# One norm of a hybrid backbone: squares summed two and two, and the latent stream's last residual put ahead of the context stream's last operand blocks

## The chip, the cores and the metric

The kernel runs on one core of a Trainium2 chip, in one launch. The metric is the device time of that launch in microseconds (us). PE is TensorE (matmul), DVE is VectorE (elementwise work and reductions), ACT is ScalarE (activations and copies), POOL is GpSimd, SP is SyncE; the last two mainly issue DMAs here. Each engine works through its own instructions in the order in which they stand, and waits on the others by semaphores.

## The reference

The network has four layers. Each holds a token mixer (layers 0 and 3 a gated DeltaNet, layer 1 differential attention, layer 2 an mLSTM) and a squared-ReLU MLP, and runs over two streams of 256 tokens with 1024 channels: the context and the latent tokens. After each of the two, a stream is updated and normalised:

```
xl = layer_norm(ALPHA * xl + m_lat[2] * yl, ln_g[i, 0], ln_b[i, 0])
xl = layer_norm(ALPHA * xl + m_lat[5] * sq_relu_mlp(modulate(xl, m_lat[3], m_lat[4]), w1[i], w2[i]),
                ln_g[i, 1], ln_b[i, 1])
if need_ctx:
    xc = layer_norm(ALPHA * xc + m_ctx[2] * yc, ln_g[i, 0], ln_b[i, 0])
    xc = layer_norm(ALPHA * xc + m_ctx[5] * sq_relu_mlp(...), ln_g[i, 1], ln_b[i, 1])

def layer_norm(x, g, b):
    mu = mean(x, -1);  var = mean(square(x - mu), -1)
    return (x - mu) * rsqrt(var + LN_EPS) * g + b
```

In layer 3 the context stream is no longer needed (`need_ctx` is false). So six places normalise both streams (two in each of the layers 0, 1 and 2), and two places in layer 3 normalise the latent stream alone.

## The kernel before

Activations lie transposed: 128 channels on the partitions, tokens along the free dimension, so a stream is 8 blocks of 128 x 256, and both streams side by side are 512 columns. All weights are split into a high and a low part, and so are the operands; a product is three passes of the PE (high x high, high x low, low x high; L201 to L203 for both streams together, L251 for one stream of 256 columns).

An output projection with its norm is `out_norm` (L706). Its first four output blocks run over both streams at once. The last four (`KEEP`) keep their weights and run once for the context half and then once for the latent half: `half(0)` and `half(1)`, 4 blocks x 8 input blocks x 3 passes = 96 passes each (L251). Each finished block is added to the residual `xa` (`residual`, L607), and summed into `acc` for the mean.

The norm is a generator, `layer_norm` (L615). It yields numbers, and `beside` (L699) puts that many passes of a fill between its steps. While the context norm is written, the fill is `half(1)`, the latent half of the same projection. While the latent norm is written, the fill is the context half of the next projection's first four blocks (`proj_first`, L221), again 96 passes. After that the latent half of those blocks follows. So the PE's order is fixed by hand in this region (`manual_schedule`), and what the norm needs from DVE and ACT must be ready when the PE comes to it.

The steps of one norm are: the mean, two matmuls against a matrix of 1/1024, one with `acc` (L620) and one with the last block of `xa` (L622); four subtractions of the mean, each over two blocks (128 x 512); four squares on ACT (L645); a sum of the squares on DVE; the variance, matmuls of the summed squares against the same matrix (L652); rsqrt by ACT and DVE; and then `emit_h` (L558), which makes the next projection's operands in four pairs of blocks p = 0 to 3: multiply by r (`xa<-xa,rs`), scale and shift (`hh`, `hf` on ACT and DVE), and the low part (`hl<-hf,hh`). The low part of pair p is written after the multiply and the scale of pair p + 1.

These DVE instructions all go through `dve` (L691), which chains each behind the one before, in the order in which the Python code issues them. They all stand at line L694 in the profile, so tile names tell them apart. The generator `norm(1, first)` gets the rest of the context norm as `other`: what the context norm had not issued when the fill ran out is issued inside the latent norm, after its four subtractions.

`NORM` holds the numbers that are yielded: `NORM[2]` = 12 passes between the mean and the subtractions, `NORM[6]` = 18 before the variance, `NORM[5]` = 20 before the operands, `NORM[4]` = 12 after each pair of operands. `VADD` says which of the four squares take in the one before: with 1, 2 and 3 all four end in one sum. Outside such regions a scheduler with a timeline of its own orders the instructions.

Of the kernel before, what the change touches and what calls it, by code (L numbers as in the profile page):

```python
# [62 lines left out]
APRI = 200  # L63
STAGS = "sds"
RPRI = 100
NORM = 0, 1, 12, 0, 12, 20, 18
VADD = 1, 2, 3
HACT = 1,
RACT = 1,
TAGS = "dddo"  # L70
# [50 lines left out]
class Net:  # L121
# [436 lines left out]
    def emit_h(self, xs, p0, s, aff, act, r=None, step=2):  # L558
# [3 lines left out]
        def low(t, hi, lo):  # L562
            for i in range(0, 2, step):
                e = slice(i, i + step)
                self.behind[1:] = [self.dve("tensor_tensor", out=lo[:, e], in0=t[:, e], in1=hi[:, e].bitcast(F32), op=ALU.subtract)]

        todo = None
        for p, x in enumerate(xs, p0):
# [16 lines left out]
            todo = t, hi, lo  # L585
            yield NORM[4]
        low(*todo)
# [27 lines left out]
    def layer_norm(self, li, lnk, s, acc, aff, act, spill=None, other=(), alone=False):  # L615

        nc = self.nc
        mu = self.ps("mu", "s")[:, CTX]
        yield NORM[0]
        nc.tensor.matmul(mu, self.onesd, acc, start=True, stop=False)  # L620
        yield NORM[1]
        nc.tensor.matmul(mu, self.onesd, self.xs(s, 7), start=False, stop=True)  # L622
        var = self.ps("var", "s")[:, CTX]
        blocks = lambda t, n: t.rearrange("p (b t) -> p b t", b=n)
        over = lambda t, n: t.unsqueeze(1).to_broadcast([P, n, NS])
        yield NORM[2]
        step = 1 if alone else 2
        for b in range(0, 8, step):
            x = blocks(self.xs(s, b, step), step)
            self.dve("tensor_tensor", out=x, in0=x, in1=over(mu, step), op=ALU.subtract)  # L630
        for _ in other:
            pass
        if alone:
            for b in range(8):
                if b % 4 == 0:
                    sqs = self.u("sq")
                sq = sqs[:, NS * (b % 4):NS * (b % 4 + 1)]
                nc.scalar.activation(sq, self.xs(s, b), AF.Square)
                nc.tensor.matmul(var, self.onesd, sq, start=b == 0, stop=b == 7)  # L639
                yield 1  # L640
        else:
            sq = [self.u("sq") for _ in range(2)]
            sq = [t[:, c] for t in sq for c in (LO, HI)]
            for p in range(4):
                nc.scalar.activation(sq[p], self.xs(s, 2 * p, 2), AF.Square)  # L645
                if p in VADD:
                    self.dve("tensor_tensor", out=sq[p], in0=sq[p - 1], in1=sq[p], op=ALU.add)
            ps = [p for p in range(4) if p + 1 not in VADD]
            for n, p in enumerate(ps):
                yield NORM[3] if n < len(ps) - 1 else NORM[6]  # L650
                for i in range(2):
                    nc.tensor.matmul(var, self.onesd, sq[p][:, STREAM[i]], start=p == ps[0] and i == 0, stop=p == 3 and i == 1)  # L652

        rt = self.u("rs", NT)
        r, t = rt[:, CTX], rt[:, LAT]
        nc.scalar.activation(r, var, AF.Ln, bias=self.bias[LN_EPS])
        nc.scalar.activation(r, r, AF.Exp, scale=-0.5)
        nc.scalar.activation(t, r, AF.Square)
        self.dve("scalar_tensor_tensor", out=t, in0=var, scalar=LN_EPS, in1=t, op0=ALU.add, op1=ALU.mult)
        self.dve("scalar_tensor_tensor", out=r, in0=t, scalar=-3.0, in1=r, op0=ALU.add, op1=ALU.mult)  # L660
        yield NORM[5]
        base = (li * 2 + lnk) * 8
        if act is None:
            for b in range(8):
                x = self.xs(s, b)
                nc.vector.scalar_tensor_tensor(out=x, in0=x, scalar=self.lng[:, base + b:base + b + 1], in1=r, op0=ALU.mult, op1=ALU.mult)
                nc.scalar.activation(x, x, AF.Identity, bias=self.par("ln_b", base + b))
                nc.sync.dma_start(out=self.out[:, b], in_=x)
        else:
            yield from self.emit_h([self.xs(s, b, 2) for b in range(0, 8, 2)], 0, s, aff, act, r, step)  # L670

        def rest(i):

            with ExitStack() as q:
                for e in self.behind:
                    q.enter_context(self.tc.issue_after(e))
                for b in range(4 * i, 4 * i + 4):
                    x = self.xs(s, b)
                    g, c = (a[:, base + b:base + b + 1] for a in (self.lnag, self.lnab))
                    if b % 2 in RACT:  # L680
                        nc.scalar.activation(x, x, AF.Identity, bias=c, scale=g)
                    else:
                        nc.vector.tensor_scalar(out=x, in0=x, scalar1=g, scalar2=c, op0=ALU.mult, op1=ALU.add)
                if spill is not None:
                    nc.gpsimd.dma_start(out=spill[:, 4 * i:4 * i + 4, STREAM[s]], in_=blocks(self.xs(s, 4 * i, 4), 4))

        if act is not None:
            for i in range(2):
                self.later(1 + i, rest, i)
# [1227 lines left out]
```

## Time and profile before

| | |
|---|---|
| time, three runs | 2708.55, 2710.31, 2710.56 us; median 2710.31 |
| the profiled execution | 2708.96 us, of which its span is 2707.1 |
| PE busy | 2529.4 us (93% of the span) |
| DVE busy | 1756.8 us (65%) |
| ACT busy | 1302.3 us (48%) |
| PE waits for `mu` on DVE (`xa`) | 16.7 us in six waits |
| PE waits for `var` on DVE (`sq`) | 11.2 us in ten waits |
| mean granted PE clock | 0.97 of full speed |

Matmuls are pipelined, so a row's duration is longer than the step to the next row: 128 x 256 passes last 0.28 us and start every 0.12 us. What counts on the PE is the time from one start to the next. A wait is the idle time of an engine in front of an instruction, put down to what ended last before it. The granted clock is 1.00 at 2.4 GHz and 0.50 at 1.2 GHz.

### The profile page before, as it was taken

Reading aid. Unit: us, or ns where it says so; the run is one execution under the profiler, and the core shown is the slowest. Engines: PE = TensorE matmul, PEld = TensorE weight load, DVE = VectorE, ACT = ScalarE, POOL = GpSimd, SP = SyncE. Lnnn points to the kernel's source line nnn. Section 1 sums busy time; section 2 is a strip of 40 time slices with the busy share of each in tenths; the row PEclk is TensorE's granted clock in tenths of the full one; section 3 lists DMA queues with packets and bytes.
Section 4 is the critical chain, followed back from the end, with each engine's and each line's share of the span. In section 5 each row is a group of like instructions: output and inputs, shape, how many; then the busy total and the mean of one; then the engine's idle time right before and its main releaser. Section 6 shows DMA issues by size and latency. Waiting matters only on the chain. (4 is left out here: it accounts for less than half of the span.)

```text
span 2707.1 us, 40474 instructions
## 1 busy us (share of the span) xinstructions
PE 2529.4 (93%) x15596; PEld 2101.9 (78%) x15596; DVE 1756.8 (65%) x3697; ACT 1302.3 (48%) x2521; POOL 180.5 (7%) x319
## 2 busy tenths in 40 slices
PE   8998798999999997999999999899999998878998
PEld 4776697887788765888778877788888876677997
DVE  4798867656646556775664546575554778866555
ACT  4545485533245345543324534362254554546654
POOL 0110020000000000000000000000021011001000
PEclk9998899999999998999999999999999998999999
DMA  7576342354541321244544134324498277533454
GB/s 275 186 266 208 113 149 94 125 163 156 162 145 65 133 102 63 94 128 160 159 160 140 63 135 155 116 80 150 143 344 318 79 248 285 216 131 125 130 185 131
DMA packets 118418, 424.86 MB, mean 157 GB/s; under 512 B 13512, under 2 KB 15560, under 8 KB 118224
## 3 DMA queue, kind: packets, MB, share of 16 engines
q1 hardware_dynamic: 83168, 296.78, 32.2%
q0 software_dynamic: 34768, 124.75, 13.5%
q8 instruction: 123, 2.02, 0.3%
q10 hardware_dynamic: 288, 0.73, 0.1%
q14 instruction: 71, 0.58, 0.1%
HBM read 378.09 MB, written 44.12 MB: 156 GB/s over the span
## 5 line engine op out<-in xcount | busy, mean ns | idle before, releaser
L189 ACT CAST whi<-raw 128x1024 fp32r<-128x1024 f32 x340 | 355.5, 1049 | 789.7 <-PE psd L202 722.9
L190 DVE TENSOR_TENSOR wlo<-raw,whi 128x1024 fp32r<-128x1024 f32 x340 | 416.3, 1225 | 297.7 <-ACT whi L189 297.2
L201 PE MATMUL psd<-hh,whi 128*128 128x512 f32 (+1 forms) x1552 | 584.8, 377 | 16.4 <-DVE z L1374 11.9
L203 PE MATMUL psd<-hh,wlo 128*128 128x512 f32 (+1 forms) x1552 | 580.3, 374 | 1.8 <-DVE wlo L190 1.8
L202 PE MATMUL psd<-hl,whi 128*128 128x512 f32 (+1 forms) x1552 | 581.7, 375 | 0.0
L201 PEld LDWEIGHTS psd<-hh,whi 128*128 128x128 f32 x1552 | 296.0, 191 | 77.6 <-DVE z L1374 12.6
L201 PE MATMUL psd<-u,whi 128*128 128x512 f32 (+1 forms) x928 | 337.6, 364 | 5.1 <-ACT whi L189 5.1
L203 PEld LDWEIGHTS psd<-hh,wlo 128*128 128x128 f32 x1552 | 295.7, 191 | 55.4 <-DVE wlo L190 2.6
L203 PE MATMUL psd<-u,wlo 128*128 128x512 f32 (+1 forms) x928 | 336.5, 364 | 2.3 <-DVE wlo L190 2.0
L202 PEld LDWEIGHTS psd<-hl,whi 128*128 128x128 f32 x1552 | 296.0, 191 | 52.0 <-issue 1.7
L202 PE MATMUL psd<-u,whi 128*128 128x512 f32 (+1 forms) x928 | 336.3, 363 | 0.0
L694 DVE SCALAR_TENSOR_TENSOR xa<-psd,mod,xa 128x256 f32<-128x256 f32 x280 | 125.9, 479 | 215.9 <-PE psd L203 187.9
L201 PEld LDWEIGHTS psd<-u,whi 128*128 128x128 f32 x928 | 174.4, 188 | 39.9 <-ACT whi L189 10.8
L203 PEld LDWEIGHTS psd<-u,wlo 128*128 128x128 f32 x928 | 174.3, 188 | 35.5 <-DVE wlo L190 6.4
L202 PEld LDWEIGHTS psd<-u,whi 128*128 128x128 f32 x928 | 174.5, 188 | 29.5
L471 DVE SCALAR_TENSOR_TENSOR rowp<-wrow,silr 128x1024 bf16<-128x1024 f32 x160 | 191.7, 1219 | 0.1
L307 DVE TENSOR_TENSOR u<-relu,u 128x512 fp32r<-128x512 f32 (+1 forms) x128 | 79.1, 624 | 49.8 <-ACT u L306 49.8
L445 POOL DMA_DIRECT2D wrow<-in_w_mod_rows_dram x80 | 42.4, 530 | 746.5 <-DVE rowp L471 617.8
L958 DVE SCALAR_TENSOR_TENSOR kq<-conv,convh,kq 128x510 f32<-128x510 f32 (+3 forms) x128 | 85.8, 687 | 5.8 <-ACT kq L951 5.3
L251 PE MATMUL psd<-hh,khi 128*128 128x256 f32 (+1 forms) x248 | 73.8, 306 | 3.5 <-ACT hh L578 3.5
L411 PE MATMUL modps<-wm,sil 128*32 128x512 f32 x448 | 65.4, 623 | 12.3 <-DVE sil L336 6.8
L251 PE MATMUL psd<-hl,khi 128*128 128x256 f32 (+1 forms) x248 | 75.6, 306 | 0.1
(408 smaller groups left out, 4508.2 us busy)
## 6 DMA issues: line engine op xcount, KB each, us to landing
raw<-in_w_dram SPq DMA_DIRECT2D x256, 512.0 KB, 3.7
wm<-in_w_mod_dram SPq DMA_DIRECT2D x112, 512.0 KB, 6.4
wrow<-in_w_mod_rows_dram POOLq DMA_DIRECT2D x80, 512.0 KB, 4.5
raw<-in_w_in_a_dram SPq DMA_DIRECT2D x41, 512.0 KB, 5.2
wpre<-in_w_in_a_dram POOLq DMA_DIRECT2D x20, 512.0 KB, 6.6
pre<-wphi POOLq DMA_DIRECT2D x20, 512.0 KB, 6.0
pre<-wpre POOLq DMA_DIRECT2D x20, 512.0 KB, 6.4
whi<-pre SPq DMA_DIRECT2D x20, 512.0 KB, 4.9
```

Source lines behind the costliest of these rows:

```text
L189: nc.scalar.copy(hi, raw)
L190: self.low = nc.vector.tensor_tensor(out=lo, in0=raw, in1=hi.bitcast(F32), op=ALU.subtract).ins
L201: nc.tensor.matmul(ps[:, c], hi[:, s], rh[:, c], start=k == 0, stop=False)
L202: nc.tensor.matmul(ps[:, c], hi[:, s], rl[:, c], start=False, stop=False)
L203: self.mm = nc.tensor.matmul(ps[:, c], lo[:, s], rh[:, c], start=False, stop=k == 7).ins
L251: self.mm = self.nc.tensor.matmul(ps[:, c], lhs[:, c128(k)], rhs[:, c], start=k == 0 and i == 0, stop=k == 7 and i == len(todo) - 1).ins
L307: self.nc.vector.tensor_tensor(out=lo, in0=src, in1=hi.bitcast(F32), op=ALU.subtract)
L411: mm.append(nc.tensor.matmul(self.mps[r:r + 32, :], self.sil[:, 2 * g + i, 6 - 2 * u:38 - 2 * u], ws[g][:, 512 * i:512 * i + 512], start=u ...
L445: self.behind_mm(self.nc.gpsimd.dma_start(out=w, in_=self.ins["w_mod_rows"][ROWMOD.index(li), b]))
L471: nc.vector.scalar_tensor_tensor(out=out, in0=self.row_w, scalar=0.5, in1=self.silr[s], op0=ALU.mult, op1=ALU.mult, accum_out=self.mod[li] ...
L694: i = getattr(self.nc.vector, name)(**k).ins
L958: nc.vector.scalar_tensor_tensor(out=y3[:, :, o], in0=x3[:, :, i], scalar=tap(t), in1=y3[:, :, o], op0=ALU.mult, op1=ALU.add)
```

## The change

Three edits. `VADD` drops the 2, so the squares are summed in two pairs (0 + 1 and 2 + 3) instead of all four, and the variance becomes matmuls over two summed tiles: two more matmuls of 128 x 256 in each norm. The yield before them is 18 passes for the first tile and 0 for the second (`NORM[6]` and `NORM[3]`). `NORM[4]` goes from 12 to 16: the context norm then has issued only pairs 0, 1 and 2 when the fill's 96 passes run out (0 + 1 + 12 + 18 + 20 + 16 + 16 = 83, and the third 16 would make 99), where before it had issued all four (51 + 12 + 12 + 12 = 87). And the latent norm takes one step of `other` just ahead of its subtractions, which is pair 3 with the low part of pair 2.

```diff
-NORM = 0, 1, 12, 0, 12, 20, 18
-VADD = 1, 2, 3
+NORM = 0, 1, 12, 0, 16, 20, 18
+VADD = 1, 3
@@ layer_norm
         yield NORM[2]
         step = 1 if alone else 2
+
+        next(iter(other), None)
         for b in range(0, 8, step):
             x = blocks(self.xs(s, b, step), step)
             self.dve("tensor_tensor", out=x, in0=x, in1=over(mu, step), op=ALU.subtract)
         for _ in other:
             pass
@@
             ps = [p for p in range(4) if p + 1 not in VADD]
             for n, p in enumerate(ps):
-                yield NORM[3] if n < len(ps) - 1 else NORM[6]
+                yield NORM[3] if n else NORM[6]
                 for i in range(2):
                     nc.tensor.matmul(var, self.onesd, sq[p][:, STREAM[i]], start=p == ps[0] and i == 0, stop=p == 3 and i == 1)
```

On DVE, at the seam from the context norm to the latent norm of layer 0's first place (`xa<-xa,rs`, `hf`, `hl` are the context's operands, `xa<-psd,mod,xa` is the latent stream's last residual, `xa<-xa,mu` the latent subtractions), the order before was

```order
L694 TENSOR_TENSOR xa<-xa,rs 128x512
L694 TENSOR_SCALAR hf<-xa,affA,affB 128x256
L694 TENSOR_TENSOR hl<-hf,hh 128x2x256
L694 TENSOR_TENSOR xa<-xa,rs 128x512
L694 TENSOR_SCALAR hf<-xa,affA,affB 128x256
L694 TENSOR_TENSOR hl<-hf,hh 128x2x256
L694 SCALAR_TENSOR_TENSOR xa<-psd,mod,xa 128x256
L694 TENSOR_TENSOR xa<-xa,mu 128x512 x4
L694 TENSOR_TENSOR hl<-hf,hh 128x2x256
L694 TENSOR_TENSOR sq<-sq 128x512 x3
```

and with the change, where lines behind the new ones are numbered two higher, it is

```order
L696 TENSOR_TENSOR xa<-xa,rs 128x512
L696 TENSOR_SCALAR hf<-xa,affA,affB 128x256
L696 TENSOR_TENSOR hl<-hf,hh 128x2x256
L696 SCALAR_TENSOR_TENSOR xa<-psd,mod,xa 128x256
L696 TENSOR_TENSOR xa<-xa,rs 128x512
L696 TENSOR_SCALAR hf<-xa,affA,affB 128x256
L696 TENSOR_TENSOR hl<-hf,hh 128x2x256
L696 TENSOR_TENSOR xa<-xa,mu 128x512 x4
L696 TENSOR_TENSOR hl<-hf,hh 128x2x256
L696 TENSOR_TENSOR sq<-sq 128x512 x2
```

The residual moved up by three instructions, and one addition of squares is gone. The same stands in all six places; in the second one, short instructions of the attention's set-up stand between, in both kernels.

On PE, at the variance of the same context norm (`psd<-go` are the latent half's passes), it was

```order
L251 MATMUL psd<-go,klo 128x256
L251 MATMUL psd<-go,khi 128x256
L652 MATMUL var<-sq,onesd 128x256 x2
L251 MATMUL psd<-go,khi 128x256
L251 MATMUL psd<-go,klo 128x256
```

and now it is

```order
L251 MATMUL psd<-go,klo 128x256
L251 MATMUL psd<-go,khi 128x256
L654 MATMUL var<-sq,onesd 128x256 x4
L251 MATMUL psd<-go,khi 128x256
L251 MATMUL psd<-go,klo 128x256
```

The passes around it stand as before; two matmuls were added, here and in each of the other eleven norms of this kind.

Away from the norms the scheduler also placed some instructions differently, in the attention of layer 1 and in the mixer of layer 3. On POOL, in layer 3's mixer (`row` are rows of decay factors, fetched by DMA and then masked), before:

```order
L1177 DMA row<-gcd 128x1024 x2
L1111 AFFINE_SELECT row<-row 128x512 x4
L1177 DMA row<-gcd 128x1024 x2
L1111 AFFINE_SELECT row<-row 128x512 x4
L995 MEMSET W 128x1024
```

and now:

```order
L1179 DMA row<-gcd 128x1024 x2
L1113 AFFINE_SELECT row<-row 128x512 x2
L1179 DMA row<-gcd 128x1024
L1113 AFFINE_SELECT row<-row 128x512 x4
L1179 DMA row<-gcd 128x1024
L1113 AFFINE_SELECT row<-row 128x512 x2
L997 MEMSET W 128x1024
```

The third of these DMAs moved ahead of two masks; nothing was added.

## Rows read from the trace of the kernel before

**Rows 1.** The page's first part: engine, busy us, share, instructions.

```profile
PE 2529.4 (93%) x15596; PEld 2101.9 (78%) x15596; DVE 1756.8 (65%) x3697; ACT 1302.3 (48%) x2521; POOL 180.5 (7%) x319
```

**Rows 2.** The PE's waits: for what, us in total, times, longest us.

```profile
PE mu L622 <- DVE xa L694: 16.7, 6, 2.9
PE var L652 <- DVE sq L694: 11.2, 10, 1.9
```

**Rows 3.** Windows: stretch, its us, busy us per engine, granted PE clock, DMA.

```profile
467.20:480.00 12.80, 12.80 (x109) 12.75 (x109) 9.95 (x22) 10.55 (x22) 0.00 (x0) 1.00 0.00 1
500.00:812.00 312.00, 309.11 (x1359) 249.18 (x1358) 192.97 (x295) 110.44 (x143) 15.34 (x29) 1.00 0.49 158
2170.00:2490.00 320.00, 273.02 (x2626) 234.93 (x2626) 248.56 (x667) 169.70 (x429) 35.93 (x57) 0.94 0.57 204
```

**Rows 4.** Timeline of PE, context norm, layer 0: start, us, instruction, [idle before].

```profile
447.01 0.28 PE L251 MATMUL psd<-go,khi 128*128 128x256 f32 x1
448.50 1.13 PE L652 MATMUL var<-sq,onesd 128*128 128x256 f32 x4 [1.20 <-DVE sq L694]
449.27 0.47 PE L251 MATMUL psd<-go,khi 128*128 128x256 f32 x1
```

**Rows 5.** Timeline of DVE, the same norm.

```profile
443.76 2.48 DVE L694 TENSOR_TENSOR xa<-xa,mu 128x512 f32<-128x512 f32 x4 [0.79 <-PE mu L622]
446.16 2.28 DVE L694 TENSOR_TENSOR sq<-sq 128x512 f32<-128x512 f32 x3
```

**Rows 6.** Timeline of ACT, the same norm.

```profile
444.49 2.42 ACT L645 ACTIVATE sq<-xa 128x512 f32<-128x512 f32 x4 [12.54 <-DVE xa L694]
```

**Rows 7.** Timeline of PE, the latent norm of layer 3's first place.

```profile
2497.57 3.72 PE L639 MATMUL var<-sq,onesd 128*128 128x256 f32 x16 [1.77 <-ACT sq L638]
```

**Rows 8.** Timeline of DVE, layer 0, from the context norm's end into the latent norm.

```profile
458.17 0.69 DVE L694 TENSOR_TENSOR xa<-xa,rs 128x512 f32<-128x512 f32 x1
458.90 0.41 DVE L694 TENSOR_SCALAR hf<-xa,affA,affB 128x256 f32<-128x256 f32 x1
459.23 0.69 DVE L694 TENSOR_TENSOR hl<-hf,hh 128x512 fp32r<-128x512 f32 x1
459.83 0.48 DVE L694 SCALAR_TENSOR_TENSOR xa<-psd,mod,xa 128x256 f32<-128x256 f32 x1
461.10 2.48 DVE L694 TENSOR_TENSOR xa<-xa,mu 128x512 f32<-128x512 f32 x4 [0.79 <-PE mu L622]
463.50 0.68 DVE L694 TENSOR_TENSOR hl<-hf,hh 128x512 fp32r<-128x512 f32 x1
464.10 2.28 DVE L694 TENSOR_TENSOR sq<-sq 128x512 f32<-128x512 f32 x3
```

**Rows 9.** Timeline of PE, the same stretch.

```profile
457.01 0.28 PE L251 MATMUL psd<-go,klo 128*128 128x256 f32 x1
460.36 0.70 PE L622 MATMUL mu<-xa,onesd 128*128 128x256 f32 x2 [2.52 <-DVE xa L694]
...
464.33 0.28 PE L251 MATMUL psd<-hh,khi 128*128 128x256 f32 x1
466.52 1.10 PE L652 MATMUL var<-sq,onesd 128*128 128x256 f32 x4 [1.91 <-DVE sq L694]
467.27 0.47 PE L251 MATMUL psd<-hl,khi 128*128 128x256 f32 x1
```

**Rows 10.** Timeline of DVE, the sixth place (layer 2, after the MLP).

```profile
2142.62 0.68 DVE L694 TENSOR_TENSOR xa<-xa,rs 128x512 f32<-128x512 f32 x1
```

**Rows 11.** Timeline of PE, the sixth place.

```profile
2151.38 1.10 PE L652 MATMUL var<-sq,onesd 128*128 128x256 f32 x4 [0.77 <-DVE sq L694]
2152.13 0.47 PE L251 MATMUL psd<-hh,khi 128*128 128x256 f32 x1
```

**Rows 12.** Windows in the latent norms of the first, second and sixth place.

```profile
460.30:464.50 4.20, 4.14 (x32) 3.99 (x32) 3.41 (x7) 2.60 (x5) 0.00 (x0) 1.00 0.24 99
834.20:837.60 3.40, 3.40 (x14) 3.22 (x15) 2.18 (x4) 1.55 (x4) 0.00 (x0) 0.51 0.00 0
2145.00:2148.40 3.40, 3.40 (x15) 3.22 (x15) 2.44 (x5) 1.72 (x3) 0.00 (x0) 0.51 0.00 0
```

**Rows 13.** Timeline of PE, the second place.

```profile
834.18 1.20 PE L622 MATMUL mu<-xa,onesd 128*128 128x256 f32 x2 [2.88 <-DVE xa L694]
```

## The prediction

> **What bounds the kernel now.** The page's first part comes first: PE is busy 93% of the span, DVE 65%, ACT 48% [rows 1]. So time is won where PE stands still or works for nothing, and DVE counts only where PE waits for it. The PE's waits are read next. Two of their groups belong to the norms: six waits for the mean, held by the residual `xa`, 16.7 us, and ten for the variance, held by the sum of squares, 11.2 us [rows 2]. The windows then tell whether a wait removed there stays removed. From 467.2 us, where the latent variance of layer 0's first place is done, PE is busy 12.80 of 12.80 us, and 309.1 of 312 us in the MLP behind it [rows 3]: nothing else there would take the time back. So each place can be followed by itself, on the PE: when does the next pass after the variance start?
>
> All starts below are the profiled execution's, and an fp32 matmul of 128 x 256 leaves two records, so a pair over one summed tile leaves four. In the norm where 16 records stand in one row, the last ends 3.72 us after the first began, and one lasts 0.38 [rows 7, 9]: (3.72 - 0.38)/15 = 0.22 us a record, 0.89 us for a pair of matmuls. That is what each norm gets more, 12 x 0.89 = 10.7 us of PE work. It costs nothing only where PE would have waited anyway.
>
> **Context norm.** Today PE comes to the variance 0.12 us after its last pass, at 447.13, waits 1.20 us, and the next pass starts at 449.27 [rows 4]. The DVE additions run from 446.16 to 448.44 [rows 5], since they follow the four subtractions and the last follows the fourth square, which ends at 444.49 + 2.42 = 446.91 [rows 6]. With the change the first sum is one addition, from 446.16 to 446.85 (0.69 us, as another instruction of that shape, [rows 8]), so PE finds it done at 447.13 and works 0.89 us. The second addition starts behind the fourth square, at 446.95, and ends at 447.64; from the end of a sum to the matmul it takes 0.14 us (464.10 + 2.28 = 466.38 to 466.52, [rows 8, 9]). So it is ready before PE is, at 448.02, and the second pair ends PE's work there at 448.91. Gain 449.27 - 448.91 = 0.36 us. All that follows in this norm starts from the variance and moves with it.
>
> **Latent norm.** Today the residual of the last latent block starts at 459.83, behind pair 3 of the context's operands and the low part of pair 2 [rows 8]. Its input was there long before: PE's last pass of it started at 457.01 and lasted 0.28 [rows 9]. PE waits 2.52 us for this residual, then passes until 464.33, and waits 1.91 us for the squares; the next pass starts at 467.27 [rows 9]. With the change the residual stands where the multiply of pair 3 stood, at 458.17, less the 0.36 won above: 457.81. From there I take the DVE steps of the rows: residual 0.48, multiply 0.73, scale 0.33, low part 0.60 [rows 8], and the subtractions start at 459.95 instead of 461.10. They take 2.40 (461.10 to 463.50) and the low part of pair 3 another 0.60, so the first addition starts at 462.95. Its sum is ready for PE at 462.95 + 0.69 + 0.14 = 463.78, the second, one step of 0.60 later, at 464.38.
>
> PE gets the mean at 457.81 + 0.48 + 0.05 = 458.34 and needs 464.33 + 0.12 - 460.36 = 4.09 us to the variance, so it is there at 462.43 and still waits 1.35. Then come two pairs without a gap: 463.78 + 1.78 = 465.56. Gain 467.27 - 465.56 = 1.71 us, the context's 0.36 in it. The wait that goes is that for the mean, from 2.5 to about 0.9 us; what is late next is DVE's way from the subtractions to the first sum.
>
> **Six places.** In the sixth place the same two points, pair 3's multiply and the first pass after the variance, lie 2152.13 - 2142.62 = 9.51 us apart [rows 10, 11], in the first 467.27 - 458.17 = 9.10 [rows 8, 9]. The chain with the change is the same, so the sixth wins 0.41 more: 2.12 us. The six waits for the mean add up to 16.7 us [rows 2], which is 4 x 2.88 as in the second place [rows 13] and 2 x 2.6 as in the first; so I count four places like the sixth and two like the first: 4 x 2.12 + 2 x 1.71 = 11.9 us.
>
> In the second and sixth place PE's clock fell to 1.2 GHz for 3.4 us when it came back from the wait for the mean, in the first it did not [rows 12]. That costs little today: in the sixth, PE still waits 0.77 us for the squares afterwards [rows 11], so DVE's chain sets the end there, and I count nothing for a clock that stays up, apart from the later mean that is already in the 9.51.
>
> **Costed at nothing.** Pair 3's operands come later for the next projection's context passes, but these take 12 passes of 0.12 us a block and reach blocks 6 and 7 only after 72 of 96, while the variance stands after 31. The order elsewhere (the attention, layer 3's mixer, with POOL's DMA ahead of two masks) adds and removes no work; how long its waits are no row tells. I take 0, with bounds of 4 us either way, somewhat over the longest single wait of the norms, 2.9 [rows 2].
>
> The sum is made against the profiled execution, 2708.96 us: 2708.96 - 11.9 = 2697.1. The median of the runs lies 1.35 above that execution, so the forecast is 2710.31 - 11.9 = 2698.4 us. Bounds of the terms: with the shorter spacing of a residual before an instruction that does not need it (0.40 in place of 0.48) and 0.86 us a pair, about 13.4; with all six places like the first, 10.3.
>
> **Rivals.**
> - *The move does not pay, the sums alone do.* The residual, moved up, waits for its PSUM tile, and DVE's operands of the context stand behind it, so the subtractions start no earlier. Then the latent sums start at 464.10 - 0.36, the first is ready at 464.57, and the next pass starts at 466.35: 0.92 us a place, 5.5 in all, 2704.8 us. Against it: the tile is done at 457.29, 0.88 us ahead of the new place [rows 8, 9], and the 0.36 moves both. The Trainium skill, in "Perfetto Trace Analysis", section "Tensor Engine Instruction (MATMUL, LD_WEIGHTS)", says that DVE and ACT take their work strictly in order, which speaks against any instruction put ahead of others that are ready; by it alone this rival's 2704.8 would hold wherever the tile came over 2 us late, and the rows show it early.
> - *The clock.* PE now stands twice for about a us, before the mean and before the variance, and the clock falls behind the second wait. 3.4 us at half speed lose 1.7 us, now on PE's way: 6 x 1.7 = 10.2, so 2708.6 us, no change. For it: in two of the three places shown the clock fell at this seam [rows 12]. Against it: it fell after a wait of 2.88 us, and did not after waits of 2.52 and 1.91 [rows 9, 12, 13], both longer than what I expect.
> - *Slower: the new order in layer 3's mixer.* PE idles 47 us there [rows 3], in chains between DVE, ACT and POOL. If the masks, or the matmuls that were moved there, lengthen such a chain, all of it is lost. It decides from 11.9 + 5.4 = 17.3 us on, which is over a third of that idle time; at half of it, 23 us, the time is 2721 us. For it: nothing in the trace; against it: no instruction was added there.
> - *More than counted.* The clock stays up in the norms and in what follows, and the bound of 13.4 holds with 4 us from the new order: 2693 us.
>
> **How the numbers follow.** Forecast 0.73, sums alone 0.11, clock 0.07, slower 0.05, more than counted 0.04. About 0.2%, 5.4 us, is what a measurement of this kernel tells from no change. Faster by more than that: nearly all of the forecast and of the last, half of the sums alone, some of the clock: 0.83. Within: 0.13. Slower: 0.04. The range is 2691 to 2706: below it goes to 13.4 and a gain of some us elsewhere, above it takes in the sums alone.
>
> **What would show it.** Right: PE's waits for the mean fall from 16.7 to about 6 us (0.9 a place); the context norms have no wait at the variance and four more records; the latent ones a wait of about 1.3 us before the first sum; at the seam the residual stands ahead of pair 3's multiply, and the granted clock stays at 1.00 there. Wrong: a wait of DVE in front of the moved residual, a wait between the two pairs of the variance, a clock of 0.50 behind the latent variance, or a longer stretch from 2170 to 2490 us.

## The result, and the profile after

The kernel before took 2709.43 us in the median of four runs (2706.24 to 2710.56), the changed one 2693.24 (2689.98 to 2697.07): a ratio of 0.994, 95% interval 0.9927 to 0.9952. So it is 16 us faster, against the forecast's 11.9. The profiled execution of the changed kernel took 2689.98 us, its span is 2688.2. The length of a norm below is the time on PE from its first mean matmul to the first pass behind its variance. A stage (a mixer, the attention, an MLP) is the time from the end of a latent norm to the first mean matmul of the next context norm.

The page's first part, against [rows 1] (engine, busy us, share, instructions):

```profile
PE 2528.5 (94%) x15644; PEld 2104.3 (78%) x15644; DVE 1747.7 (65%) x3685; ACT 1301.1 (48%) x2521; POOL 181.0 (7%) x319
```

There are 48 more PE records (twelve norms, four each) and 12 fewer on DVE, as counted; the PE's busy time differs by under 1 us. What went is waiting. The waits of PE, against [rows 2] (for what, us in total, times, longest us):

```profile
PE mu L622 <- DVE xa L696: 6.8, 6, 1.2
PE var L654 <- DVE sq L696: 5.4, 5, 1.1
...
PE var L654 <- DVE lamt L1551: 1.2, 1, 1.2
```

The six waits for the mean fell from 16.7 to 6.8 us. Of the ten waits for the variance six lay in the context norms and four in latent ones. Now the context norms have none, and all six latent norms have one: five are in the second line, and that of the second place is in the last, put down to another instruction of DVE (as a wait of 0.9 us there was before). The context norm of layer 0's first place on PE, against [rows 4] (start, us, instruction, idle before):

```profile
444.40 0.28 PE L251 MATMUL psd<-go,khi 128*128 128x256 f32 x1
444.52 1.89 PE L654 MATMUL var<-sq,onesd 128*128 128x256 f32 x8
446.06 0.47 PE L251 MATMUL psd<-go,khi 128*128 128x256 f32 x1
```

PE goes into the variance 0.12 us after the last pass, as into any other matmul, and both pairs are through in 446.06 - 444.52 = 1.54 us. The DVE at the seam, against [rows 8]:

```profile
454.36 0.69 DVE L696 TENSOR_TENSOR hl<-hf,hh 128x512 fp32r<-128x512 f32 x1
454.96 0.48 DVE L696 SCALAR_TENSOR_TENSOR xa<-psd,mod,xa 128x256 f32<-128x256 f32 x1
455.36 0.68 DVE L696 TENSOR_TENSOR xa<-xa,rs 128x512 f32<-128x512 f32 x1
456.08 0.41 DVE L696 TENSOR_SCALAR hf<-xa,affA,affB 128x256 f32<-128x256 f32 x1
456.41 0.69 DVE L696 TENSOR_TENSOR hl<-hf,hh 128x512 fp32r<-128x512 f32 x1
457.01 2.48 DVE L696 TENSOR_TENSOR xa<-xa,mu 128x512 f32<-128x512 f32 x4
459.40 0.69 DVE L696 TENSOR_TENSOR hl<-hf,hh 128x512 fp32r<-128x512 f32 x1
460.00 1.29 DVE L696 TENSOR_TENSOR sq<-sq 128x512 f32<-128x512 f32 x2
```

The moved residual has no wait in front of it, and neither have the subtractions, which waited 0.79 us for the mean before: the three instructions that the residual passed now cover that. The PE there and in the sixth place, against [rows 9] and [rows 11]:

```profile
455.50 0.70 PE L622 MATMUL mu<-xa,onesd 128*128 128x256 f32 x2 [0.88 <-DVE xa L696]
...
460.84 1.97 PE L654 MATMUL var<-sq,onesd 128*128 128x256 f32 x8 [1.09 <-DVE sq L696]
462.45 0.47 PE L251 MATMUL psd<-hl,khi 128*128 128x256 f32 x1
...
2126.63 0.70 PE L622 MATMUL mu<-xa,onesd 128*128 128x256 f32 x2 [1.23 <-DVE xa L696]
...
2131.97 1.97 PE L654 MATMUL var<-sq,onesd 128*128 128x256 f32 x8 [1.09 <-DVE sq L696]
2133.58 0.47 PE L251 MATMUL psd<-hh,khi 128*128 128x256 f32 x1
```

Two waits of about a us each stand where 2.5 to 2.9 and up to 1.9 us stood. The eight records stand in one row: no wait lies between the pairs. Windows over the latent norms of the first and sixth place, over the stretch behind the first, the MLP, and layer 3's mixer, against [rows 3] and [rows 12] (stretch, its us, busy us per engine, granted PE clock, DMA):

```profile
453.90:462.50 8.60, 6.63 (x46) 5.89 (x44) 7.32 (x14) 5.60 (x10) 0.00 (x0) 1.00 0.44 154
2124.60:2133.60 9.00, 6.67 (x44) 5.93 (x44) 7.75 (x14) 6.88 (x11) 0.00 (x0) 1.00 0.00 0
462.45:475.25 12.80, 12.80 (x109) 12.77 (x108) 10.03 (x22) 10.61 (x22) 0.00 (x0) 1.00 0.00 1
495.20:807.20 312.00, 309.11 (x1360) 249.15 (x1359) 193.06 (x295) 110.38 (x143) 15.89 (x30) 1.00 0.48 158
2151.45:2471.45 320.00, 276.74 (x2627) 239.14 (x2626) 249.23 (x667) 168.78 (x429) 35.56 (x57) 0.93 0.56 203
```

The clock stays at 1.00 in the sixth place, where it was 0.51; the MLP behind is as dense as before (309.11 of 312 in both), so nothing took the gain back there. In layer 3's mixer the change moved nothing of weight: from the sixth place's variance to the next norm it is 342.2 us in both traces.

By places, before and after: the six context norms fell from 6.98 or 6.99 us to between 6.35 and 6.38, 3.7 us in all; the latent ones from 10.14, 11.19, 11.16, 11.02, 10.25, 11.02 to 8.55, 9.14, 9.00, 8.99, 8.65, 9.00, 11.5 us in all. That is 15.2 us. The spans differ by 18.9; of the rest 2.6 us lie in layer 0's mixer, where the two kernels have the same instructions.

### The profile page after: what moved, and what is told of

The parts are those of the page before. It is cut to its first block, busy times and chain, and to the rows that moved or that the text cites. A ratio compares the mean times of both kernels' runs of the same rounds, so it can differ in the third digit from the quotient of the medians.

```text
span 2688.2 us, 40535 instructions
## 1 busy us (share of the span) xinstructions
PE 2528.5 (94%) x15644; PEld 2104.3 (78%) x15644; DVE 1747.7 (65%) x3685; ACT 1301.1 (48%) x2521; POOL 181.0 (7%) x319
## 3 DMA queue, kind: packets, MB, share of 16 engines
q8 instruction: 123, 2.02, 0.3%
## 5 line engine op out<-in xcount | busy, mean ns | idle before, releaser
L779 ACT ACTIVATE relu<-relu 128x512 f32<-128x512 f32 (+1 forms) x128 | 73.4, 579 | 3.3
```

Source lines behind the costliest of these rows:

```text
L779: nc.scalar.activation(r, r, AF.Square)
```

## The experiments

The theory: the change gains where PE waited for DVE's chain in the norms, and both parts are needed, since a wait that stays long lets the PE clock fall. The rivals: the sums alone are the gain; the move alone is; or the gain lies in stages outside the norms.

**Both kernels again.** No edit.

> The kernel before, profiled once more. It tells how far a stage moves by itself: the norms should repeat to 0.1 us where no stretch at 1.2 GHz falls into them, and the mixers (layers 0 to 3) by up to 3 us, as their low-clock stretches fall. If the difference of 2.6 us in layer 0's mixer, whose instructions are the same in both kernels, is chance, this run's is nearer to that of the whole change.

> The changed kernel once more, timed in five rounds on the chip of the others and profiled. Theory: the twelve norms are 15.1 us shorter than before in this profile too, no stretch at 1.2 GHz in any of the six seams; the ratio to before stays at 0.9945 +- 0.001. Rival (the first comparison was luck in the mixers): the norms' 15 us are partly lost elsewhere and the ratio comes out above 0.996.

The kernel before, one execution: 2713.13 us; context norms 6.98 or 6.99, latent ones 10.68, 10.68, 11.13, 11.14, 10.79, 11.14 us; layer 0's mixer 441.4 (442.3 in the first trace), layer 3's 346.1 (342.2). The changed one: 2693.25 us, five runs, ratio 0.9937 (0.9925 to 0.9949); every norm within 0.03 us of the first trace, layer 0's mixer 442.3. So the changed kernel's norms repeat. The context norms of before do too, but its latent ones differ by up to 0.5 us a place, as the stretches at 1.2 GHz fall: 64.8 us together in the first trace, 65.5 in the second. By the second traces the twelve norms are 16.0 us shorter, by the first 15.2. The 2.6 us in layer 0's mixer were chance. Layer 3's mixer differs by some us from execution to execution, and the attention by 2.0 and the mLSTM by 1.1 between the two traces of before; smaller differences there mean nothing below.

**The sums alone.** From the kernel before:

```diff
-VADD = 1, 2, 3
+VADD = 1, 3
-                yield NORM[3] if n < len(ps) - 1 else NORM[6]
+                yield NORM[3] if n else NORM[6]
```

> The sums alone: squares summed in pairs, two pairs of variance matmuls, but the residual in its old place. My theory: the edits work by themselves. Context norm, from the first mean matmul to the next pass after the variance: 6.4 us as with the whole change (before 7.0). Latent norm, the same stretch: first sum ready at 7.8 us, two pairs of 0.77 behind it, so 9.35 us in the first place (before 10.14) and about 10.2 in those like the sixth (11.0). The waits for the mean stay at 2.5 to 2.9 us and the clock still falls behind them in most places. In all 3.7 + about 4 us won, so about 7 to 8 us faster than before. Rival (PE-bound): each of the 12 norms pays for its two added matmuls and the kernel is up to 9 us slower.

Measured: 2708.08 us, ratio 0.9994 (0.9983 to 1.0005): no change, where I expected 7 to 8 us. The context norms give their 0.62 us each. The latent ones are 9.38, 11.80, 10.84, 11.69, 9.53 and 12.10: shorter than in the first trace of before by 0.7 us in places 1 and 5 and by 0.3 in place 3, longer by 0.6, 0.7 and 1.1 in places 2, 4 and 6. The mean of the second place on PE, and windows over the same point of places 2 and 6:

```profile
830.80 1.22 PE L622 MATMUL mu<-xa,onesd 128*128 128x256 f32 x2 [2.88 <-DVE xa L695]
```

```profile
829.50:832.90 3.40, 2.10 (x8) 1.92 (x9) 2.09 (x5) 1.54 (x4) 0.00 (x0) 0.50 0.00 0
2140.20:2143.60 3.40, 2.74 (x11) 2.56 (x12) 2.09 (x5) 1.54 (x4) 0.00 (x0) 0.50 0.00 0
```

The wait for the mean is as long as before, and the clock falls to 1.2 GHz in it, in places 2, 3, 4 and 6 (for 6.8 us, in place 3 for 3.4). In the kernel before, PE that came late to the variance only shortened its wait there. Now the sum is ready early, PE has no wait left there in these four places (0.3 us in the other two), and the slow passes are on its way.

**The move alone.** From the changed kernel:

```diff
-VADD = 1, 3
+VADD = 1, 2, 3
```

> The move alone: last latent residual ahead of pair 3, but all four squares in one sum. My theory: context norms stay at 7.0 us. In the latent norm the mean comes 1.3 to 1.7 us earlier, the third addition is ready 1.2 us after the place where the first sum is ready with the whole change, and one pair follows: 8.9 us in the first place, about 9.35 in those like the sixth, against 10.14 and 11.0. The clock stays at 2.4 GHz at the seams. About 9 us faster than before. Rival (the wait only moves): the latent norms stay within 0.3 us of before, no change.

Measured: 2707.9 us, ratio 0.9997 (0.9987 to 1.0007): no change. The latent norms are 5.8 us shorter together (9.26, 9.80, 9.72, 10.46, 10.03, 9.72), but the clock did not stay up, and the MLPs of layers 0 and 2 are 1.5 us longer each. The first place's variance on PE, and windows behind it and behind the fifth's:

```profile
462.74 1.27 PE L654 MATMUL var<-sq,onesd 128*128 128x256 f32 x4 [2.67 <-DVE sq L696]
```

```profile
463.50:466.90 3.40, 3.40 (x17) 3.32 (x16) 1.38 (x3) 1.31 (x3) 0.00 (x0) 0.51 0.00 0
1777.70:1781.10 3.40, 3.32 (x11) 2.99 (x12) 0.00 (x0) 1.17 (x3) 0.00 (x0) 0.50 0.02 5
```

The long wait went from the mean to the variance (2.67 us), and behind it the clock is at 0.50 while PE has work without a gap: 3.4 us at half speed are 1.7 us lost. Pass by pass against the changed kernel, layer 0's MLP loses its 1.5 us wholly in its first passes; layer 2's loses 0.8 there and 0.7 evenly along the rest, at a granted clock of 1.00. Behind the latent norms the clock is low for 3.4, 1.4, 1.8 and 3.4 us in places 1, 4, 5 and 6. Half of that, 5.0 us, is an estimate of what the stages behind lose, and it takes back most of the 5.8. The attention, the mLSTM and layer 3's mixer were also 1.6, 1.0 and 3.5 us longer than in the first trace of before; the mLSTM and the mixer are no longer than in the second (241.0 and 346.1), the attention is.

**Pair 3 not ahead of the subtractions.** From the changed kernel:

```diff
-        next(iter(other), None)
```

> The whole change without the one step of the context's rest ahead of the latent subtractions: pair 3 with its low parts comes behind the four subtractions and ahead of the additions. My theory: the subtractions start about 0.85 us earlier, but ACT does the four squares first and then pair 3's three activations, so the low part of pair 3, and the first addition behind it, come about 1.4 us later than with the whole change: latent norms 10.0 us in the first place, 10.4 in those like the sixth; 8 to 9 us slower than the whole change, about 6 us faster than before. Rival: only the number 16 matters, no difference to the whole change.

Measured: 2709.83 us, ratio 1.0007 (0.9997 to 1.0016). The latent norms are 11.1 to 11.7 us, longer than before in each place (by 4.4 us together) and by over a us than I expected. DVE and ACT in the first place show why:

```profile
456.50 2.48 DVE L695 TENSOR_TENSOR xa<-xa,mu 128x512 f32<-128x512 f32 x4 [0.79 <-PE mu L622]
458.90 0.68 DVE L695 TENSOR_TENSOR xa<-xa,rs 128x512 f32<-128x512 f32 x1
```

```profile
459.62 1.09 ACT L578 ACTIVATE hh<-xa,affB,affA 128x256 fp32r<-128x256 f32 x2 [3.73 <-DVE xa L695]
460.62 0.59 ACT L580 ACTIVATE hf<-xa,affB,affA 128x256 f32<-128x256 f32 x1
461.11 2.17 ACT L646 ACTIVATE sq<-xa 128x512 f32<-128x512 f32 x4
```

ACT stands 3.73 us in front of pair 3's activations, whose multiply on DVE now follows the subtractions. The squares are behind them, though the first of the four subtractions was done about 2 us earlier; I had expected the squares first. (The Trainium skill, in "Perfetto Trace Analysis", section "Tensor Engine Instruction (MATMUL, LD_WEIGHTS)", has it that ACT takes its work strictly in order; these rows agree.) PE waits 3.1 us for the variance in every place, and the clock falls behind it in all six, of which this is the first:

```profile
464.40:467.80 3.40, 3.40 (x15) 3.13 (x14) 0.46 (x2) 1.31 (x3) 0.00 (x0) 0.50 0.00 0
```

So `next(other)` is no detail: without it, in this order, sums and move together give nothing.

**Useless work in the wait.** The sums alone, with four matmuls between the two mean matmuls of each latent norm, into a PSUM part that nobody reads (`vt` is the variance's tile, which is allocated a few lines earlier for that); nothing is left out:

```diff
+        vt = self.ps("var", "s")
+        var = vt[:, CTX]
+        if s and not alone:
+            for _ in range(4):
+                nc.tensor.matmul(vt[:, LAT], self.onesd, acc, start=True, stop=True)
```

> The sums alone, as in e1_sums, with four useless matmuls of 128 x 256 (into a part of PSUM that nobody reads) on PE between the two matmuls of the latent mean, where PE waits 2.5 to 2.9 us for the residual anyway: about 1.7 us of pure extra PE work in each of six places, 10 us in all. Theory (the clock): the waits are too short then for the clock to fall at the seam, so no latent norm holds a stretch at 1.2 GHz; 9.4 us in the first and fifth place as in e1_sums, 10.2 in the other four, where e1_sums took 10.8 to 12.1. In all some 5 us faster than e1_sums, in spite of the added work. Rival (the clock does not matter, the places were slow for another reason): the four places stay at 10.8 us and more, or grow by the added work.

Measured: 2702.33 us, ratio 0.997 (0.9959 to 0.9981): PE has 24 matmuls more than with the sums alone (48 records, at 0.22 us each an estimated 10 us of work), and the kernel is 5.7 us faster. Against the kernel before, timed beside each, the ratio goes from 0.9994 to 0.997, which is 6.5 us. The second place on PE, and a window over that norm:

```profile
827.43 1.89 PE L626 MATMUL var<-acc,onesd 128*128 128x256 f32 x8
830.47 0.70 PE L627 MATMUL mu<-xa,onesd 128*128 128x256 f32 x2 [1.15 <-DVE xa L699]
835.10 2.00 PE L657 MATMUL var<-sq,onesd 128*128 128x256 f32 x8 [0.37 <-DVE sq L699]
```

```profile
826.80:836.80 10.00, 8.48 (x52) 7.43 (x52) 8.47 (x21) 5.80 (x11) 0.00 (x0) 1.00 0.01 2
```

The mean comes at the same distance as with the sums alone, 3.7 us behind the first mean matmul; all that differs is that PE worked in between. The clock stays up in all six places, and the latent norms are 9.96, 9.82, 9.81 and 9.82 us in places 2, 3, 4 and 6, against 11.80, 10.84, 11.69 and 12.10. In places 1 and 5, where the clock had not fallen, the work changes nothing (9.32 and 9.49). This shows the clock as what ate the gain of the sums in the latent norms.

**The same work in the kernel before.** The same lines:

> The kernel before, with four useless 128x256 matmuls between the two mean matmuls of each latent norm (into a part of a PSUM tile that nobody reads; nothing is left out). They take about 1.7 us of PE in a wait of 2.5 to 2.9 us. Theory (a long wait lets the clock fall, and in the kernel before this costs little since DVE's chain sets the end): the half-clock stretches in the latent norms go (before: 3.4, 6.8, 3.4, 3.4, 3.4 us in places 2 to 6), the latent norms take 10.1 to 10.6 us instead of 10.1 to 11.2, some 2.5 us in all: 2707 to 2708 against 2710, a ratio of about 0.999, while the same filling gave 5.7 us on the kernel with the sums alone. Rival A (the clock is worth as much here as there): 2704.5, 0.998. Rival B (the filling gives nothing but its own work): slower by up to 10 us.

Measured: 2718.67 us, ratio 1.0031 (1.0018 to 1.0043). My expectation failed; rival B has the sign, but not the reason, since the added work lies in the waits and makes the norms shorter. The second place on PE, and windows before and behind that variance:

```profile
834.66 0.70 PE L627 MATMUL mu<-xa,onesd 128*128 128x256 f32 x2 [1.15 <-DVE xa L698]
...
840.80 1.53 PE L656 MATMUL var<-sq,onesd 128*128 128x256 f32 x4 [1.89 <-DVE nlam L1557]
```

```profile
834.00:840.80 6.80, 4.26 (x33) 4.00 (x33) 6.01 (x16) 3.41 (x7) 0.00 (x0) 1.00 0.01 2
841.40:844.80 3.40, 3.40 (x16) 3.22 (x15) 0.00 (x0) 2.37 (x3) 0.00 (x0) 0.50 0.00 0
```

The clock no longer falls at the mean, so PE comes to the variance earlier, waits 1.8 to 1.9 us there, and the clock falls behind that instead, in five of six places. The latent norms are 1.4 us shorter together than in the first trace of before, but the MLPs of layers 0 and 2 are 1.4 and 1.8 us longer and the mLSTM 2.2. Layer 0's MLP loses it wholly in its first passes, layer 2's 1.1 us of it; the other 0.7 is spread along the stage. All this is some 4 us of the 10 by which this execution is longer than that trace. In layer 3's mixer it took 349.4 us, 7.2 more than there and 3 above the longest in any other kernel here (339 to 346 us). The mean granted clock of that mixer was 0.90, against 0.95 and 0.92 in the two traces of before, but at 0.92 it took 339.0 us in one kernel and 346.2 in another, so the clock alone doesn't tell its length. So the falls moved to where work follows, and that explains less than half of the loss; the rest stays open.

**The same work where the move leaves a wait.** The move alone, with the four matmuls just ahead of the latent variance's:

```diff
@@ layer_norm, ahead of the variance's matmuls
+                if s and not alone:
+                    for _ in range(4):
+                        nc.tensor.matmul(vt[:, LAT], self.onesd, acc, start=True, stop=True)
```

> The move alone, with four useless 128x256 matmuls just ahead of the latent variance's matmuls, where the move alone leaves a wait of 2.7 us on PE (into a part of a PSUM tile that nobody reads; nothing is left out). Theory (what the move alone wins is taken back by the clock, which falls to 1.2 GHz behind that wait): the wait before the variance falls to about 1 us, no stretch of half clock follows it, the latent norms take 9.3 to 9.8 us in all six places instead of 9.3 to 10.5, and the MLPs of layers 0 and 2, 1.5 us longer each with the move alone, come back to 347.6 and 343.1 us: 2703 to 2705, a ratio of 0.998 against 0.9997 of the move alone. Rival (the longer MLPs and norms have another cause): no change from the move alone, or slower by the work added.

Measured: 2708.43 us, ratio 0.9991 (0.998 to 1.0001): by time neither the expectation nor clearly more than the move alone. By places it came in part. Behind the first variance, and behind the sixth place's mean:

```profile
468.20:471.60 3.40, 3.32 (x24) 3.21 (x25) 0.73 (x3) 1.31 (x3) 0.00 (x0) 1.00 0.00 0
2144.10:2147.50 3.40, 3.40 (x17) 3.33 (x17) 3.36 (x7) 3.25 (x6) 0.00 (x0) 0.50 0.00 0
```

Behind the variance the clock stays up everywhere, and the MLPs of layers 0 and 1 are back at 347.5 and 347.8 us; layer 2's came back halfway, 343.8. Its first passes lose nothing any more, and what is left, 0.65 us, is spread evenly along the stage, just as in the sums filled (343.8 too): it isn't the fall. The latent norms are 9.17, 9.77, 9.65 and 9.33 in places 1, 2, 3 and 5. In places 4 and 6 the clock fell behind the mean, after a wait of 1.23 us that does no harm in the changed kernel, and they are 10.1. The attention, the mLSTM and layer 3's mixer are again 1.0 to 3.3 us longer than in the first trace of before, as with the move alone; against the second only the attention is (3.6 us). So the clock is shown as the reason of the longer first passes behind the variance. That it took back the whole gain of the move isn't shown: without those falls, with latent norms 6.7 us shorter than before, the kernel gained 2.4 us by the ratio (0.9991), which isn't told from nothing, and why not more is open.

**Pair 3 wholly behind the sums.** From the changed kernel: `next(other)` goes, and `for _ in other: pass` stands behind the additions instead of behind the subtractions.

```diff
-        next(iter(other), None)
-        for _ in other:
-            pass
@@ behind the additions of the squares
+            for _ in other:
+                pass
```

> The whole change, with the context's rest (pair 3, and the low parts of pairs 2 and 3) put behind the two additions of squares of the latent norm instead of ahead of the subtractions. DVE then only has the residual, four subtractions and two additions before the variance, and does pair 3 while ACT works on the reciprocal root. My theory: DVE's way sets the variance, so the first sum is ready about 1.3 us earlier and the second is ready when PE wants it: latent norms about 7.3 us in the first place and 7.8 in those like the sixth, 7 to 8 us faster than the whole change. Rival (the work is needed there): pair 3's activations stand ahead of the logarithm on ACT, the reciprocal root comes up to 0.8 us late, PE waits for the latent operands or for pair 3, and nothing is won.

Measured: 2693.42 us, ratio 0.9944 (0.9929 to 0.9958), the same as the whole change. The latent norms are as expected, 7.2 to 7.8 us, without any wait for the variance: 8.1 us less than with the whole change. But the MLPs are 0.8, 1.2 and 0.9 us longer than after, the mLSTM 3.1, the attention 2.6, layer 3's mixer 3.6. Part of it is seen: pair 3's operands come late, and PE waits for them near the start of the next stage (1.1 us at 841.67, and 1.0 us more waiting in layer 1's MLP).

**Only its low part behind the sums**, in two spellings with the same order on DVE and PE in the norms and MLPs (the first is shown; the second puts the two lines behind the variance's matmuls):

```diff
-        for _ in other:
-            pass
@@ behind the additions of the squares
+            for _ in other:
+                pass
```

> The whole change with one line moved: the low part of pair 3 (one DVE instruction) behind the two additions of squares instead of ahead of them. Theory: it takes 0.60 us out of DVE's way to the first sum, and the second sum is ready when PE is done with the first pair, so each latent norm is 0.55 us shorter (8.0 us in the first place, 8.45 in those like the sixth) and, unlike with all of pair 3 moved, nothing new stands ahead of the logarithm on ACT, so the stages behind stay as they are: 3.3 us faster than the whole change. Rival: the squares on ACT set the sums, so the norms stay within 0.1 us of the whole change.

> The whole change, with the low part of the context's pair 3 behind the two additions, written another way than in the run before (the order on DVE and PE is the same). If the longer MLPs of that run belong to this order (0.9 us in layer 0's, 0.4 in layer 2's), they show again, at a granted clock of 1.00 and with no new wait; if they were chance, the MLPs are back at 347.6, 347.7 and 343.1 us. The latent norms are 0.6 us shorter than with the whole change in either case.

Measured: 2695.62 us (0.9948, 0.9935 to 0.9961), and 2701.77 in the one execution of the second. The latent norms are 0.6 us shorter each than after, as expected, in both; and in both layer 0's MLP is 0.9 us longer (348.45 and 348.48, against 347.55 and 347.53 in the changed kernel's two traces). So that repeats and is no chance of one execution; whether the order itself makes it, or something that comes with it, isn't shown. The 3.6 us that the norms give don't reach the time (2693.25 for the changed kernel beside it). From 480 to 800 us PE is busy 317.1 of 320 us at a clock of 1.00 in these kernels and in the changed one: it isn't waiting. The 0.9 us grow evenly along the stage (0.2 after a quarter, 0.4 after half). By line and form, the group that grew in the run with pair 3 wholly late, against the changed kernel ahead of it (busy us, mean ns):

```profile
L201 PE MATMUL psd<-hh,whi 128*128 128x512 f32 x224 | 87.8, 392 | 0.0
```

```profile
L201 PE MATMUL psd<-hh,whi 128*128 128x512 f32 x224 | 88.9, 397 | 0.0
```

224 passes of 5 ns more are 1.1 us; the other two passes over `hh` and `hl` change by -0.4 and +0.2. What makes them longer stays open. In layer 2's MLP the like is seen without this order too (0.65 us in the sums filled and in the move filled). No version beats the whole change.

The latent norms of the kernels side by side (waits in us; falls of the clock to 1.2 GHz in the six places, at the mean / at or behind the variance):

| | wait for mean | wait for variance | falls | six latent norms, us | ratio |
|---|---|---|---|---|---|
| before | 2.5 to 2.9 | up to 1.9 | 5 / 0 | 64.8 | 1 |
| sums alone | 2.5 to 2.9 | up to 0.35 | 4 / 0 | 65.3 | 0.9994 |
| move alone | 0.9 to 1.2 | 2.7 (one 1.2) | 1 / 4 | 59.0 | 0.9997 |
| change without `next` | 0.9 to 1.2 | 3.1 to 3.2 | 0 / 6 | 69.2 | 1.0007 |
| sums, filled | 0.8 to 1.2 | 0.2 to 0.4 | 0 / 0 | 58.2 | 0.997 |
| before, filled | 0.8 to 1.2 | 1.8 to 1.9 | 0 / 5 | 63.4 | 1.0031 |
| move, filled | 0.8 to 1.2 | up to 1.0 | 2 / 0 | 58.1 | 0.9991 |
| whole change | 0.9 to 1.2 | 1.1 to 1.2 | 0 / 0 | 53.3 | 0.994 |
| low part of pair 3 late | 0.9 to 1.2 | 0.5 to 0.6 | 0 / 0 | 49.7 | 0.9948 |
| pair 3 wholly late | 0.8 to 1.2 | none | 0 / 0 | 45.2 | 0.9944 |

## Why the prediction was right, and where its terms were off

**The mechanism held at each step.** The residual found its tile done (no wait at 454.96), the subtractions were no longer held by the mean, the context norm has no wait, PE's waits in the latent norm are 0.9 to 1.2 and 1.1 to 1.2 us (forecast 0.9 and 1.35; the 1.35 runs from the last pass's start + 0.12, and by the profile's count, from the pass's end, it is 1.19), the two pairs follow without a gap, and the clock stays at 1.00. Four places gain about 2.0 of their own, two 1.6, in the grouping that was read off the waits.

**The size was too small: 15.2 us in the norms instead of 11.9.** The term that was most off is the price of a pair of variance matmuls, 0.89 us. It was worked out from sixteen records in a row [rows 7], where 0.22 us is right for one record behind another. But the first pair replaces the pair of before, and that one's price stood in [rows 4]: 448.50 to 449.27, 0.77 us, since the next pass starts just behind the last record and not a whole step later. Two pairs take 1.54 us with no wait ahead of them (444.52 to 446.06) and 1.61 behind a wait (460.84 to 462.45), not 1.78. (The Trainium skill, in "Perfetto Trace Analysis", section "Tensor Engine Instruction (MATMUL, LD_WEIGHTS)", says that the end times of PE's records are a model. No run here can check that; what is counted here are starts.) That is 0.24 in each context norm (0.60 for 0.36) and 0.17 in each latent one.

The second term is the moved residual: DVE's next instruction started 0.40 us behind it (454.96 to 455.36), the spacing that the text had put into the bounds, not 0.48. With it the first latent place closes: 1.35 forecast without the context's share, + 0.17 + 0.08 = 1.60; measured 1.59. The sixth: 1.76 + 0.25 = 2.01; measured 2.02. Over six places these two terms give 6 x (0.24 + 0.17 + 0.08) = 2.9 of the 3.3 us that were missing.

The norms' 15.2 us lie above the text's own upper bound too. That bound, 13.4, comes to 13.1 by its terms (11.9 + 6 x 0.08 for the residual + 6 x 4 x 0.03 for the pairs). The time of 2693.24 us still fell into the stated range, since that range left room for some us won elsewhere, which did not come: that part is luck.

**The rival "sums alone"** was priced at 5.5 us; it gave 1.6 by the ratio, which is no change. Its mechanism (a wait in front of the residual) did not occur; but its price was worked out with a clock that plays no part, and this is where the text erred: "that costs little today" was nearly right of the kernel before (place 1 took 10.14 us without a fall and 10.68 with one in the two traces), and wrong as soon as DVE's chain is shorter, where a fall costs 1.0 to 2.3 us a place (sums alone against the same with filled waits).

**The rival "clock"** named the right mechanism and price: a fall behind the variance is on PE's way and costs up to 1.7 us. At the changed kernel's waits of up to 1.2 us it did not come; it did come at 1.8 to 1.9 (before, filled), at 2.7 and at 3.1. The argument against it, waits of 2.52 and 1.91 us in the first place without a fall, was thinner than it looked: in the second trace of before that place did fall. And in the two kernels with the move alone and filled the clock fell behind waits of 1.23 us too. So the margin of the change was smaller than the text had it, and that the clock stayed up was in part luck. The change shortens both waits of the latent norm and removes that of the context norm; which of these keeps the clock up was not tested one by one.

**Slower through layer 3's mixer** did not come: 342.2, and 342.2 and 342.1 us. **"Taken as 0"**, the stages elsewhere: the spans without the twelve norms are 2600.4 and 2603.9 us in the two traces of before and 2596.7 and 2600.0 in those of the changed kernel, so any difference lies inside what single executions vary by.

## What to carry to other kernels

Two long waits of the same engine behind one another are one thing: shortening only one leaves a standstill that can cost the gain again through the clock, so follow the engine to the next wait and ask how long that one becomes. Take a price from the row where that very instruction stands between its neighbours, from its start to the next instruction's start, before deriving it from a longer row. When an instruction is moved behind others on one engine, look at the engine that serves it too: ACT waited 3.7 us for operands that had been put later on DVE, with its squares behind them.

## What the runs showed of the hardware

- The PE's clock fell to 1.2 GHz, for 3.4 or 6.8 us at a time, in or behind 25 of the 29 waits of 2.5 to 3.2 us in the latent norms of five traces (before twice, sums alone, move alone, change without `next`). It never fell in the twelve latent norms of the changed kernel's two traces, with waits up to 1.23 us, nor in the 24 of the sums filled and of the three kernels with pair 3 or its low part late. In the two kernels with the move alone and filled it fell at a mean wait of 1.23 us in three of twelve; there the context norm still had a wait of 1.2 us before its variance. Whether that wait is the reason was not tested. A wait's length alone doesn't decide it: the first place of the kernel before had no fall in one trace and one in the other.
- Useless matmuls in a wait made a kernel faster by 5.7 us (2708.08 to 2702.33), and the same matmuls made another slower by 8 (2710.19 to 2718.67). There the fall moved to a point with work behind it, which explains less than half of the loss.
- With pair 3 or its low part behind the sums, the MLP of layer 0 took some 0.25% longer (348.3 to 348.5 us for 347.5), evenly along the stage, at a granted clock of 1.00 and without a new wait inside it, in three kernels; why is open.
